# A mixture-of-experts stage whose first 28 experts add their results to the tokens in DRAM

## The chip, the cores and the metric

The kernel runs on one core of a Trainium2 chip. The metric is the device time in microseconds (us) of one execution. The core has TensorE (PE, matmuls; PEld is its weight load), VectorE (DVE), ScalarE (ACT), GpSimd (POOL) and SyncE (SP); SP issues nearly all transfers, GpSimd the indirect ones, and sixteen DMA engines carry them.

## What is computed

One encoder layer on 512 tokens of width 1024, in float32: a state-space mixer beside a latent attention, a cross-attention into 256 memory tokens, then a mixture of 32 gated experts, and a last norm. The change lies in the expert part:

```python
h = _rms(x, norm_moe_g[l])
x = x + _hier_moe(...)
return _rms(x, norm_final_g)

# _hier_moe, for the 512 tokens t = h:
#   the best of 4 groups, then the best 2 of the 8 experts of that group
eid = g_idx[:, None] * MOE_PER_GROUP + top_i
gates = jnp.sum(jax.nn.one_hot(eid, MOE_EXPERTS) * top_w[..., None], axis=1)
for g in range(MOE_GROUPS):
    sl = slice(g * MOE_PER_GROUP, (g + 1) * MOE_PER_GROUP)
    a = silu(einsum('td,edf->tef', t, w_gate[sl])) * einsum('td,edf->tef', t, w_up[sl])
    a = a * gates[:, sl, None]
    out = out + einsum('tef,efd->td', a, w_down[sl])
```

Each token has two experts. An expert has 3 MB of weights (gate and up 1024 x 256 each, down 256 x 1024), so the 32 experts have 96 MB, each byte read once.

## The kernel before

**Tiling.** The 32 experts are worked in 16 pairs n = 0..15. An expert has 64 places (`CAP`) for tokens; a pair fills the 128 partitions, its first expert in partitions 0 to 63, its second in 64 to 127. Tables worked out on the chip say for each place which token sits there (`TK`, and `IX` as integers; an empty place has a number out of range), with which weight (`GT`) and with which norm factor (`RS`). The stream X before this part lies in four SBUF tiles `X[t]` of 128 tokens x 1024 (called xr in the trace), and a copy of it lies in DRAM as `hd`, written by `logit_T` (L1322).

**One pair.** `gather(n)` (L1674) is an indirect DMA by GpSimd that brings the pair's rows of `hd` to `XG[n % 2]`; places out of range are skipped. `get` transposes them (pX), VectorE multiplies by the gain (XT). `first(n)` (L1755) runs 32 matmuls (pG) with gate and up, then silu on ScalarE (sl) and the product on VectorE (a). `second(n)` (L1793) transposes that (pA, aT), runs 16 matmuls with the down weights into two halves (pD), and writes the result times the gate weight as a pair of a high and a low half, `Y` (ScalarE L275, VectorE L276). It also makes `oht`, the 0/1 matrix that says which place belongs to which token.

**The sum.** Y stands by place, X by token. `combine` (L1814) takes two pairs at a time, n-2 and n-1 at each even n >= 2: for each of the four token tiles and two halves of the width four matmuls with `oht` sum high and low halves of both pairs in PSUM (pC), and VectorE adds that to X (L1824): 32 matmuls and 8 additions. Pairs 14 and 15 are summed in the end part by `last_sum` (L1859), followed by `fin_`: an addition per tile and half ("a"), its sum of squares and the root ("s"), the scaling and the store ("o"); `TO` (L66) is the order of these steps, shared out over VectorE, ScalarE and GpSimd.

**Weights and places.** Weights come in loads of 1 MB (gate and up of half an expert's width as two transfers, down as one) into a ring of SBUF places named by tags: earlier tiles of the layer (A, KV, H, Z, E, G), `NF` places F, and two places Y at first. `ring` (L1261) is the order in which places come round, `ahead` how many loads have a place before the first pair is done, `turn` the order of the first loads. `load_to(k)` issues loads up to the k-th on SP's queue; each waits until the place's last reader is done. `load_to` is called after each pair. `late` splits the last two down loads into halves of the width.

**What sets the order.** A scheduler orders the instructions on each engine by the program's order and its priorities, and adds the semaphore waits. `behind` pins one instruction behind another on an engine. On TensorE a pair's matmuls follow the pair before; between them stands the sum of two pairs.

Of the kernel before, what the change touches and what calls it, by code (L numbers as in the profile page):

```python
# [10 lines left out]
F32 = mybir.dt.float32  # L11
# [54 lines left out]
TO = 'a00 s00 a01 s01 a10 a11 o01 s10 o00 s11 a20 a21 o11 s20 o10 s21 a30 a31 o21 s30 s31 o20 o31 o30'.split()  # L66
# [18 lines left out]
NF = 1  # L85
# [11 lines left out]
GP = 0  # L97
TP = 0
# [5 lines left out]
def build(tc, I, out, dbg=None, stop=None):  # L104
# [872 lines left out]
    def ua(shape, dt, name):  # L977
        return A.tile(shape, dt, name=name, tag="A")
# [233 lines left out]
    hd = DR.tile([S, D], F32, name="hd")  # L1212
# [51 lines left out]
    tags += tuple(ring[i % len(ring)] for i in range(108 - ahead))  # L1264
    free = iter(tags[96:])

    turn = [5, 4, 20] + [i for i in range(ahead) if tags[i] not in "EFGY"]
    nheld = len(turn)
    turn += [6, 7] + list(range(ahead - NF, 96))

    def slot(tag, shape, name):
        if tag == "A":
            return ua(shape, F32, name)
        if tag in "EG":
            return (E[0] if tag == "E" else GP_).tile(shape, F32, name=name, tag=tag)
        if tag in "FY":
            return MP.tile(shape, F32, name=name, tag=tag, bufs=NF if tag == "F" else 2)
        return u(tag, shape, F32, name)
# [3 lines left out]
    def load_to(n):  # L1282
        while nld[0] < min(n, 96):
# [4 lines left out]
            after = nheld + 2 + FE < nld[0] <= ahead  # L1288
# [6 lines left out]
            else:  # L1295
# [3 lines left out]
                if i == 94:  # L1299
                    late.append((t, e))  # L1300
                    nc.sync.dma_start(t[:, :, 0:512], wdn[e][:, :, 0:512])
                elif i == 95:
                    late.append((t, e))
                    nc.sync.dma_start(t[:, :, 0:512], wdn[e][:, :, 0:512])
                    for t_, e_ in late:
                        nc.sync.dma_start(t_[:, :, 512:D], wdn[e_][:, :, 512:D])
                elif nld[0] == nheld + 2 + FE and FH:
                    nc.sync.dma_start(t[:, :, 0:512], wdn[e][:, :, 0:512])
                    held.append((t, e))
                else:  # L1310
                    nc.sync.dma_start(t, wdn[e])
            ew[e, c] = t

    late, gat, held = [], [], []
# [191 lines left out]
    load_to(nheld + 2 + min(FE, NF))  # L1506
# [67 lines left out]
    GT, RS = RC.tile([128, 16], F32, name="GT"), RC.tile([128, 16], F32, name="RS")  # L1574

# [17 lines left out]
    def weights(w, j):  # L1593
# [6 lines left out]
        v.tensor_tensor(fi[:, 1], w[:, :, 2], es_[:, cs], OP.not_equal)  # L1600
        v.tensor_tensor(fi, fi, w4[:, :, 0:2].rearrange("p n q -> p q n"), OP.mult)
# [78 lines left out]
    for t, e in held:  # L1680
        behind(nc.gpsimd.memset(t[0:1, 0, 512:513], 0.0), gat[-1])
        nc.sync.dma_start(t[:, :, 512:D], wdn[e][:, :, 512:D])
# [56 lines left out]
    silu = [None]  # L1739
# [53 lines left out]
    def second(n):  # L1793
# [6 lines left out]
        Y = MP.tile([128, 2, D], F32R, name=f"Y{n}", tag="Y")  # L1800
        oht = MP.tile([128, S], F32R, name=f"oht{n}", tag="oht")
        v.tensor_scalar(oht, tokh, TK[:, n:n + 1], None, OP.is_equal)
        stage["y", n] = Y, oht
        yield at_i
        for c in range(2):
# [6 lines left out]
            yield split(Y[:, 0, c * 512:c * 512 + 512], Y[:, 1, c * 512:c * 512 + 512], pd, GT[:, n:n + 1])[0]  # L1812

    def combine(ns, cs=(0, 1)):  # L1814
        for t in range(NT):
            for c in cs:
                ps = bank(f"pC{ns[0]}{t}{c}")
                for i, n in enumerate(ns):
                    Y, oht = stage["y", n]
                    for h in range(2):  # L1820
                        nc.tensor.matmul(ps, oht[:, t * 128:t * 128 + 128], Y[:, h, c * 512:c * 512 + 512],  # L1821
                                         start=i == 0 and h == 0, stop=i == len(ns) - 1 and h == 1)
                o = X[t][:, c * 512:c * 512 + 512]
                v.tensor_tensor(o, o, ps, OP.add)  # L1824

    fst = C.tile([128, 4, NT], F32, name="st_fin")
    for n in range(16):
# [19 lines left out]
        load_to(ahead + 4 - 2 * min(n, 1) + 6 * n - LS)  # L1847
        if n >= 2 and n % 2 == 0:
            combine((n - 2, n - 1))
# [26 lines left out]
    def fin_(k, t, c):  # L1876
        x = X[t][:, half[c]]
        r = fst[:, 3, t:t + 1]
        if k == "a":
            turn_("v", v.tensor_tensor(x, x, pc[t, c], OP.add))  # L1880
            if c == 0:
                nc.gpsimd.tensor_tensor(xg0[:, t], x, gf[:, half[0]], OP.mult)
# [6 lines left out]
        elif c:  # L1889
            turn_("v", v.reciprocal(r, r))  # L1890
            turn_("v", v.scalar_tensor_tensor(xg1[:, t], x, r, gf[:, half[1]], OP.mult, OP.mult))
            nc.sync.dma_start(out[0, t * 128:t * 128 + 128, half[1]], xg1[:, t])
        else:
            if FP >> t & 1:
                nc.gpsimd.tensor_scalar(xg0[:, t], xg0[:, t], r, 1.0, OP.mult, OP.mult)
            else:
                turn_("a", nc.scalar.activation(xg0[:, t], xg0[:, t], AF.Copy, scale=r))
            nc.sync.dma_start(out[0, t * 128:t * 128 + 128, half[0]], xg0[:, t])
# [29 lines left out]
```

## Time and profile before

| | |
|---|---|
| time, median of 3 runs (least to most) | 754.31 us (751.39 to 755.1) |
| the profiled execution | 754.67 us |
| its span, first to last instruction | 752.9 us |
| TensorE busy in the span, mean granted clock | 716.8 us (95%), 0.98 |
| VectorE, ScalarE, GpSimd busy | 450.3, 267.5, 76.6 us |
| DMA moved | 154.06 MB, mean 205 GB/s |
| chain that ended last: TensorE, VectorE, DMA | 77%, 13%, 3% |
| matmuls of the sums (L1821), in the chain | 53.8 us busy, 7% |

How to read it: the expert stage runs from about 484 us to the end, and the means over the span hide it. In its stretches one looks at TensorE's busy time and granted clock (1.00 is 2.4 GHz), at the DMA share (1.0: all sixteen engines busy) and at GB/s; then at the chain of waits, to see which of two busy resources the other waits for. Matmul times overlap, so a line's busy time is the union of its matmuls, not their number times their mean.

### The profile page before, as it was taken

The numbers are of one execution on the slowest core, as the hardware profiler recorded it, in microseconds if no ns is written. First come the engines' busy times: TensorE is split into PE (matmuls) and PEld (weight loads), VectorE is DVE, ScalarE is ACT, GpSimd is POOL, SyncE is SP. The second block draws the span as 40 slices with busy tenths as digits, with TensorE's granted clock in tenths as the row PEclk, the third lists the DMA queues.
The fourth block names the chain that finished last, engine by engine and source line by source line (L and its number), as shares of the span: only waits on it lengthen the run. The fifth ranks groups of instructions, "written<-read, shape, count | busy, mean of one in ns | idle before, by whom it ended". The sixth has DMA issues, their size and how long they took to land.

```text
span 752.9 us, 10637 instructions
## 1 busy us (share of the span) xinstructions
PE 716.8 (95%) x3900; PEld 504.7 (67%) x3900; DVE 450.3 (60%) x1018; ACT 267.5 (36%) x539; POOL 76.6 (10%) x135
## 2 busy tenths in 40 slices
PE   6999988997999999999999999999999999999994
PEld 4787777876688888888887888745353553535443
DVE  4799997955677878544557335545355543524245
ACT  5652255342756756434445222121112011111124
POOL 6200002013200000102000002200100001000003
PEclk9999999999989999999999999999999999999998
DMA  7673130543341533323258966599999999999003
GB/s 208 171 208 96 42 103 23 163 115 90 98 114 43 157 111 127 97 84 85 84 201 301 318 219 218 190 375 397 381 411 399 410 408 412 410 412 361 31 1 114
DMA packets 94592, 154.06 MB, mean 205 GB/s; under 512 B 29244, under 2 KB 61088, under 8 KB 90697
## 3 DMA queue, kind: packets, MB, share of 16 engines
q1 hardware_dynamic: 92120, 149.19, 56.6%
q0 software_dynamic: 2400, 4.15, 1.7%
q8 instruction: 32, 0.52, 0.3%
q14 instruction: 24, 0.19, 0.1%
q10 hardware_dynamic: 16, 0.00, 0.0%
HBM read 150.40 MB, written 6.82 MB: 209 GB/s over the span
## 4 chain that ended last, share of the span: by engine, by line
PE 77%; DVE 13%; DMA 3%; ACT 2%; issue 2%; SPq 1%; POOL 1%; ACTq 0%; DVEq 0%
PE pG L1763 15%; PE pD L1809 8%; PE pC L1821 7%; PE po L1023 2%; DVE lo L213 2%; PE pX L1430 2%; PE pX L1747 2%; PE pxq L267 2%; PE pxq L266 2%; PE pxq L265 2%; PE pxo L265 2%; PE pxo L266 2%; PE pxo L267 1%; PE pPT L1012 1%; DMA raw<-w_in 1%
## 5 line engine op out<-in xcount | busy, mean ns | idle before, releaser
L1763 PE MATMUL pG<-gu,XT 128*64 128x512 f32 x512 | 116.0, 596 | 0.0
L213 DVE TENSOR_TENSOR lo<-raw,hi 128x1024 fp32r<-128x1024 f32 (+3 forms) x64 | 75.8, 1189 | 59.7 <-ACT hi L203 59.3
L203 ACT ACTIVATE hi<-raw 128x1024 fp32r<-128x1024 f32 (+3 forms) x64 | 63.9, 1002 | 101.5 <-issue 21.5
L1763 PEld LDWEIGHTS pG<-gu,XT 128*64 128x64 f32 x512 | 35.5, 137 | 65.2 <-issue 63.4
L1782 ACT ACTIVATE sl<-pG,RS 128x256 f32<-128x256 f32 x16 | 7.6, 475 | 150.8 <-PE pG L1763 150.8
L1809 PE MATMUL pD<-dn,aT 128*64 128x512 f32 x256 | 60.6, 599 | 0.0
L1784 DVE SCALAR_TENSOR_TENSOR a<-pG,RS,sl 128x256 f32<-128x256 f32 x16 | 10.7, 671 | 74.3 <-ACT sl L1782 56.9
L1821 PE MATMUL pC<-Y,oht 128*128 128x512 f32 x224 | 53.8, 396 | 0.0
L1821 PEld LDWEIGHTS pC<-Y,oht 128*128 128x128 f32 x224 | 41.4, 188 | 15.0 <-issue 6.5
L1824 DVE TENSOR_TENSOR xr<-xr,pC 128x512 f32<-128x512 f32 x56 | 38.1, 686 | 6.7 <-PE pC L1821 6.7
L276 DVE SCALAR_TENSOR_TENSOR Y<-pD,GT,Y 128x512 fp32r<-128x512 f32 x32 | 24.0, 749 | 29.9 <-ACT Y L275 29.7
L275 ACT ACTIVATE Y<-pD,GT 128x512 fp32r<-128x512 f32 x32 | 22.0, 687 | 49.8 <-PE pD L1809 49.8
L1809 PEld LDWEIGHTS pD<-dn,aT 128*64 128x64 f32 x256 | 17.9, 136 | 30.4 <-issue 28.1
L1675 POOL DMA_INDIRECT XG<-hd,IX x15 | 15.5, 1032 | 189.1 <-PE pX L1747 185.1
L1404 DVE TENSOR_TENSOR XT<-pX,gmo 128x512 f32<-128x512 f32 x32 | 21.9, 686 | 12.4 <-PE pX L1747 8.3
L266 PE MATMUL pxq<-gT,hi 128*128 128x512 f32 x64 | 25.6, 400 | 0.0
L265 PE MATMUL pxq<-gT,hi 128*128 128x512 f32 x64 | 25.5, 399 | 0.0
L267 PE MATMUL pxq<-gT,lo 128*128 128x512 f32 x64 | 25.4, 396 | 0.0
L1747 PEld LDWEIGHTS pX<-ident,XG 128*128 128x128 f32 x120 | 16.2, 192 | 8.6 <-issue 7.3
L265 PE MATMUL pcq<-hT,hi 128*128 128x512 f32 x48 | 19.3, 402 | 2.8 <-DVE s_t L592 2.8
L266 PE MATMUL pq<-lo,cq 128*128 128x384 f32 x48 | 18.2, 379 | 2.3 <-DVE lo L213 2.3
L1007 ACT ACTIVATE P<-psc,sm 128x128 f32<-128x128 f32 (+3 forms) x32 | 16.8, 528 | 7.3 <-DVE sm L1006 7.1
(608 smaller groups left out, 1700.0 us busy)
## 6 DMA issues: line engine op xcount, KB each, us to landing
gu<-moe_w_gate SPq DMA_DIRECT2D x64, 512.0 KB
gu<-moe_w_up SPq DMA_DIRECT2D x64, 512.0 KB
dn<-moe_w_down SPq DMA_DIRECT2D x30, 1024.0 KB
raw<-w_in SPq DMA_DIRECT2D x9, 512.0 KB
raw<-xattn_w_v SPq DMA_DIRECT2D x8, 512.0 KB
raw<-xattn_w_k SPq DMA_DIRECT2D x8, 512.0 KB
raw<-w_out SPq DMA_DIRECT2D x8, 512.0 KB
raw<-xattn_w_q SPq DMA_DIRECT2D x8, 512.0 KB
```

The costliest lines, as they stand in the source:

```text
L203: anchor["act"] = nc.scalar.activation(hi, r, AF.Copy)
L213: anchor["dve"] = nc.vector.tensor_tensor(lo, r, hi.bitcast(F32), OP.subtract)
L265: i = nc.tensor.matmul(o, lh, rh, start=start, stop=False)
L266: nc.tensor.matmul(o, lh, rl, start=False, stop=False)
L267: anchor["pe"] = nc.tensor.matmul(o, ll, rh, start=False, stop=stop)
L275: i = nc.scalar.activation(hi, src, AF.Copy, scale=g)
L276: j = nc.vector.scalar_tensor_tensor(lo, src, g, hi.bitcast(F32), OP.mult, OP.subtract)
L1747: i = nc.tensor.transpose(ps[:, k * 128:k * 128 + 128], xg[:, 4 * c + k], ident)
L1763: i = nc.tensor.matmul(pg[64 * s:64 * s + 64], xt[c][:, kk, 64 * s:64 * s + 64], ew[2 * n + s, c][:, :, kk], start=k == 0, stop=k == 7)
L1809: i = nc.tensor.matmul(pd[64 * s:64 * s + 64], at_[:, f, 64 * s:64 * s + 64], ew[2 * n + s, 2][:, f, c * 512:c * 512 + 512], start=f == 0, ...
L1821: nc.tensor.matmul(ps, oht[:, t * 128:t * 128 + 128], Y[:, h, c * 512:c * 512 + 512], start=i == 0 and h == 0, stop=i == len(ns) - 1 and h ...
L1824: v.tensor_tensor(o, o, ps, OP.add)
```

## The change

The results of pairs 0 to 13 (`NS = 14`) no longer go through `oht` and TensorE. A second copy of X, `xd`, is written to DRAM beside `hd`. `second(n)` writes the result as one float32 half of a tile `YY` (ScalarE alone, no low half), and GpSimd issues two indirect DMAs with `compute_op=OP.add` that add the 128 rows to `xd`. Two, because a token may sit in both experts of a pair: the first takes the rows that are a token's first choice, the second those that are its second choice; `IY` holds the index lists, in which the other rows have a number out of range and are skipped. `combine` is gone. At n = 14 `take_back` reads `xd` into new tiles `xb`, which stand for X from then on. Pairs 14 and 15 are summed on TensorE as before.

X's four SBUF tiles hold weights meanwhile: two places X join the ring, `NF` is 2, and Y has one place for the first load in place of two. In the end part the scaling of the first halves moves from ScalarE and GpSimd to VectorE, and `TO` has another order.

```diff
-TO = 'a00 s00 a01 s01 a10 a11 o01 s10 o00 s11 a20 a21 o11 s20 o10 s21 a30 a31 o21 s30 s31 o20 o31 o30'.split()
+TO = 'a00 s00 a01 s01 a10 s10 a11 s11 o00 o01 a20 s20 a21 s21 o10 o11 a30 s30 a31 s31 o20 o21 o30 o31'.split()
...
-NF = 1
+NF = 2
...
+NS = 14
...
+    hd, xd = (DR.tile([S, D], F32, name=n) for n in ("hd", "xd"))
...
-    ring = ("A",) * 4 + ("E", "G") + ("A",) * (NA - 4) + ("KV",) * 4 + ("H",) * 2 + ("Z",) * 4 + ("E",) + ("F",) * NF
-    ahead = len(ring) + 2
-    tags = ring[:6] + ("Y",) * 2 + ring[6:]
+    ring = ("A",) * 4 + ("E", "G") + ("A",) * (NA - 4) + ("KV",) * 4 + ("H",) * 2 + ("Z",) * 4 + ("E",) + ("F",) * NF + ("X",) * 2
+    ahead = len(ring) + 1
+    nlate = sum(t in "FX" for t in ring)
+    tags = ring[:6] + ("Y",) + ring[6:]
...
+        nc.sync.dma_start(xd[t * 128:t * 128 + 128, n * 512:n * 512 + 512], xs)
...
+        if 2 * j < NS:
+            for w_ in range(2):
+                v.scalar_tensor_tensor(IY[:, w_, cs], fi[:, 1 - w_], EMPTY, TK[:, cs], OP.mult, OP.add)
...
-        Y = MP.tile([128, 2, D], F32R, name=f"Y{n}", tag="Y")
...
+            if not YY:
+                YY.append(slot("Y", [128, 2, D], "YY"))
+            Y = YY[0][:, n % 2]
...
+                yield nc.scalar.activation(Y[:, c * 512:c * 512 + 512], pd, AF.Copy, scale=GT[:, n:n + 1])
+        if not sums:
+
+            for w in range(2):
+                nc.gpsimd.indirect_dma_start(out=xd, out_offset=bass.IndirectOffsetOnAxis(ap=IY[:, w, n:n + 1], axis=0),
+                                             in_=Y, in_offset=None, bounds_check=S - 1, oob_is_err=False,
+                                             compute_op=OP.add)
...
-    def combine(ns, cs=(0, 1)):
...
+    def take_back():
+
         for t in range(NT):
...
+            if t % 2 == 0:
+                xb = slot(next(free), [128, 2, D], f"xb{t}")
+            nc.sync.dma_start(xb[:, t % 2], xd[128 * t:128 * t + 128])
+            X[t] = xb[:, t % 2]
...
-        if n >= 2 and n % 2 == 0:
-            combine((n - 2, n - 1))
+        if n == NS:
+            take_back()
...
+            if c == 0:
+                turn_("v", v.reciprocal(r, r))
+            xg = (xg0, xg1)[c]
+            turn_("v", v.scalar_tensor_tensor(xg[:, t], x, r, gf[:, half[c]], OP.mult, OP.mult))
```

The order of instructions shows it at three places. On GpSimd, in the middle of the stage, before the change (XG is what a gather fills; what a row waits for stands in brackets, PE, DVE and Activation being engines, DMASW0 to DMASW7 the landings of eight DMAs by GpSimd in turn):

```order
L1675 DMA XG_4703<-hd,IX 128x1024 [waits DMASW5_49,DMASW3_49,PE_49]
L1675 DMA XG_4702<-hd,IX 128x1024 [waits DMASW4_49,DMASW6_49,DVE_49,PE_49]
L1675 DMA XG_4703<-hd,IX 128x1024 [waits DMASW5_49,PE_49]
L1675 DMA XG_4702<-hd,IX 128x1024 [waits DMASW6_49,DVE_49,PE_49]
L1675 DMA XG_4703<-hd,IX 128x1024 [waits DMASW7_49,PE_49]
```

And after it (xd is the copy in DRAM, YY the result, IY the index lists):

```order
L1680 DMA XG_4713<-hd,IX 128x1024 [waits DMASW5_49,DMASW1_49,PE_49]
L1827 DMA xd<-YY,IY 512x1024 [waits DMASW6_49,DMASW4_49,Activation_49]
L1827 DMA xd<-YY,IY 512x1024 [waits DMASW6_49]
L1680 DMA XG_4712<-hd,IX 128x1024 [waits DMASW2_49,DVE_49,PE_49]
L1827 DMA xd<-YY,IY 512x1024 [waits DMASW7_49,Activation_49]
L1827 DMA xd<-YY,IY 512x1024 [waits DMASW1_49]
L1680 DMA XG_4713<-hd,IX 128x1024 [waits DMASW5_49,PE_49]
L1827 DMA xd<-YY,IY 512x1024 [waits DMASW2_49,Activation_49]
L1827 DMA xd<-YY,IY 512x1024 [waits DMASW4_49]
```

Between two gathers stand now the two additions of a pair: the first waits for ScalarE's YY and for the landing of the addition before it, the second for the landing of the first.

On TensorE, around the sum of pairs 0 and 1, before the change (dn is a down weight; two rows of down matmuls, then the first of 32 matmuls of the sum):

```order
L1809 MATMUL pD_5107<-dn_4678,aT_5095 64x512
L1809 MATMUL pD_5107<-dn_4680,aT_5095 64x512
L1821 MATMUL pC_5130<-Y_5003,oht_5004 128x512 x2
L1821 MATMUL pC_5130<-Y_5097,oht_5098 128x512 x2
L1821 MATMUL pC_5136<-Y_5003,oht_5004 128x512 x2
L1821 MATMUL pC_5136<-Y_5097,oht_5098 128x512
L1821 MATMUL pC_5142<-Y_5003,oht_5004 128x512
L1821 MATMUL pC_5136<-Y_5097,oht_5098 128x512
```

And after it:

```order
L1817 MATMUL pD_5134<-dn_4691,aT_5126 64x512
L1817 MATMUL pD_5134<-dn_4693,aT_5126 64x512
L1749 MATMUL pX_5170<-ident,XG_4713 128x128 x3
L1765 MATMUL pG_5162<-gu_4695,XT_5168 64x512
L1765 MATMUL pG_5162<-gu_4698,XT_5168 64x512
```

After the down matmuls of a pair follow the next pair's last transposes and its gate and up matmuls; the 32 matmuls of the sum are gone.

On SP, from the last weights on, before the change (novi is a count that is read into a register, fin the last gain, xg the output):

```order
L1301 DMA dn_6220<-moe_w_down 128x2x512
L1304 DMA dn_6222<-moe_w_down 128x2x512
L1306 DMA dn_6220<-moe_w_down 128x2x512
L1306 DMA dn_6222<-moe_w_down 128x2x512
L1707 TENSOR_LOAD novi
L1707 ISA x2
L1853 DMA fin<-norm_final_g 128x1024
L1898 DMA out<-xg_6534 128x512
L1892 DMA out<-xg_6535 128x512
```

And after it:

```order
L1304 DMA dn_6020<-moe_w_down 128x2x512
L1307 DMA dn_6022<-moe_w_down 128x2x512
L1309 DMA dn_6020<-moe_w_down 128x2x512
L1309 DMA dn_6022<-moe_w_down 128x2x512
L1709 TENSOR_LOAD novi
L1709 ISA x2
L1836 DMA xb_6172<-xd 128x1024 x2
L1836 DMA xb_6175<-xd 128x1024 x2
L1866 DMA fin<-norm_final_g 128x1024
L1905 DMA out<-xg_6246 128x512
L1905 DMA out<-xg_6247 128x512
```

Four reads of xd now stand ahead of the gain on SP's queue, and they wait for the last addition.

## Rows read from the trace of the kernel before

**Rows 1.** Stretches: length, busy us (instructions) by engine, granted clock, DMA share, GB/s.

```profile
core 0: us, PE busy (x) PEld busy (x) DVE busy (x) ACT busy (x) POOL busy (x), PEclk, DMA share, GB/s
...
519.10:550.60 31.50, 31.50 (x164) 15.77 (x164) 16.09 (x40) 4.63 (x10) 2.19 (x2) 1.00 1.00 394
...
614.00:645.50 31.50, 31.50 (x152) 14.97 (x148) 12.67 (x21) 4.30 (x8) 1.98 (x2) 1.00 1.02 412
```

**Rows 2.** Chain that ended last, 630 to 660 us: start, us, what.

```profile
634.48 7.02 PE pG L1763 x32
641.50 0.37 PE pA L1797 x2
641.87 0.55 PE pX L1747 x5
642.42 3.63 PE pD L1809 x16
646.05 7.50 PE pC L1821 x32
653.55 0.33 PE pX L1747 x3
```

**Rows 3.** Stretches, columns of rows 1: before the first pairs, after the weights.

```profile
484.00:487.00 3.00, 2.85 (x24) 1.07 (x23) 2.56 (x9) 0.00 (x0) 1.21 (x1) 1.00 0.00 0
487.00:490.00 3.00, 2.75 (x30) 0.99 (x26) 2.29 (x20) 0.31 (x2) 1.25 (x3) 1.00 0.67 221
...
694.00:696.00 2.00, 2.00 (x12) 0.64 (x10) 0.15 (x1) 0.69 (x1) 0.00 (x0) 1.00 0.36 135
```

**Rows 4.** DMA queues from 495 to 690 us: packets, MB, share of 16 engines.

```profile
q1 hardware_dynamic: 17387, 75.19, 97.2%
q0 software_dynamic: 1735, 3.06, 4.2%
```

**Rows 5.** The gathers' line, 495 to 690 us: ns, starts; us to landing.

```profile
L1675 POOL DMA_INDIRECT XG<-hd,IX x13: 989/992/1202, 495.3 to 685.7; - x13
...
DMA to landing us min/median/max: 6.7/7.8/8.8
```

**Rows 6.** The same line, 485 to 487 us, DMA engines idle.

```profile
DMA to landing us min/median/max: 4.6/4.6/4.6
```

**Rows 7.** Chain that ended last, whole span: a store, a load.

```profile
164.31 4.35 DMA kd<-s5k
...
173.74 3.19 DMA raw<-mla_w_kv_up
```

**Rows 8.** DMA issues of these two: engine, op, times, KB each.

```profile
raw<-mla_w_kv_up SPq DMA_DIRECT2D x4, 256.0 KB
...
kd<-s5k SPq DMA_DIRECT2D x4, 128.0 KB
```

**Rows 9.** Timeline from 505 us: start, us, engine, line, operation, idle before.

```profile
506.84 0.69 ACT L275 ACTIVATE Y<-pD,GT 128x512 fp32r<-128x512 f32 x1 [1.05 <-PE pD L1809]
...
507.57 0.99 POOL L1675 DMA_INDIRECT XG<-hd,IX  x1 [11.26 <-PE pX L1747]
```

**Rows 10.** Timeline from 708 us, columns of rows 9.

```profile
708.89 0.35 SPq L1853 DMA_DIRECT2D fin<-norm_final_g  x1
...
735.04 7.55 PE L1864 MATMUL pC<-Y,oht 128*128 128x512 f32 x32
...
744.48 0.68 DVE L1880 TENSOR_TENSOR xr<-xr,pC 128x512 f32<-128x512 f32 x1
...
745.08 0.15 DVE L1890 RECIPROCAL st_fin<-st_fin 128x1 f32<-128x1 f32 x1
...
746.47 0.75 DVE L1891 SCALAR_TENSOR_TENSOR xg<-xr,st_fin,fin 128x512 f32<-128x512 f32 x1
```

**Rows 11.** Stretches early in the span, columns of rows 1.

```profile
25.00:30.00 5.00, 3.89 (x13) 3.42 (x14) 2.18 (x12) 2.51 (x4) 2.11 (x6) 0.66 0.70 203
55.00:60.00 5.00, 2.24 (x12) 1.72 (x12) 4.93 (x28) 1.48 (x3) 0.00 (x0) 1.00 0.50 132
```

More of the change, by code (lines that the diff above doesn't have):

```diff
@@ L1260, in build, with slot @@
     order += parts(15, (2,))
[L1261 to L1264 removed]
+    ring = ("A",) * 4 + ("E", "G") + ("A",) * (NA - 4) + ("KV",) * 4 + ("H",) * 2 + ("Z",) * 4 + ("E",) + ("F",) * NF + ("X",) * 2
+    ahead = len(ring) + 1
+    nlate = sum(t in "FX" for t in ring)
+    tags = ring[:6] + ("Y",) + ring[6:]
+    tags += tuple(ring[i % len(ring)] for i in range(116 - ahead))
     free = iter(tags[96:])
[L1267 removed]
+    turn = [5, 4, 19] + [i for i in range(ahead) if tags[i] not in "EFGXY"]
     nheld = len(turn)
[L1269 to L1271 removed]
+    turn += [6] + list(range(ahead - nlate, 96))
+    def slot(tag, shape, name, dt=F32):
         if tag == "A":
[L1273 removed]
+            return ua(shape, dt, name)
         if tag in "EG":
[L1275 removed]
+            return (E[0] if tag == "E" else GP_).tile(shape, dt, name=name, tag=tag)
         if tag in "FY":
[L1277 to L1278 removed]
+            return MP.tile(shape, dt, name=name, tag=tag, bufs=NF if tag == "F" else 1)
+        return u("H" if tag == "X" else tag, shape, dt, name)
     nld = [0]
@@ L1287, in load_to @@
             tag = tags[i]
-            after = nheld + 2 + FE < nld[0] <= ahead
+            after = nheld + 1 < nld[0] <= ahead
             if c < 2:
@@ L1574, in build @@
     GT, RS = RC.tile([128, 16], F32, name="GT"), RC.tile([128, 16], F32, name="RS")
+    IY = RC.tile([128, 2, 16], I32, name="IY")
     def look_up(ohb, ps, j, cols, chain=False):
@@ L1799, in second @@
         at_i = nc.scalar.activation(at_, ps[:, 0:256].rearrange("p (f t) -> p f t", f=2), AF.Copy)
-        Y = MP.tile([128, 2, D], F32R, name=f"Y{n}", tag="Y")
-        oht = MP.tile([128, S], F32R, name=f"oht{n}", tag="oht")
-        v.tensor_scalar(oht, tokh, TK[:, n:n + 1], None, OP.is_equal)
-        stage["y", n] = Y, oht
+        sums = n >= NS
+        if sums:
+            Y = slot(next(free), [128, 2, D], f"Y{n}", F32R)
+            oht = MP.tile([128, S], F32R, name=f"oht{n}", tag="oht")
+            v.tensor_scalar(oht, tokh, TK[:, n:n + 1], None, OP.is_equal)
+            stage["y", n] = Y, oht
+        else:
+            if not YY:
+                YY.append(slot("Y", [128, 2, D], "YY"))
+            Y = YY[0][:, n % 2]
         yield at_i
@@ L1811, in second @@
                     in_turn(n, i)
-            yield split(Y[:, 0, c * 512:c * 512 + 512], Y[:, 1, c * 512:c * 512 + 512], pd, GT[:, n:n + 1])[0]
-    def combine(ns, cs=(0, 1)):
-        for t in range(NT):
[L1816 to L1824, printed above, removed]
+            if sums:
+                yield split(Y[:, 0, c * 512:c * 512 + 512], Y[:, 1, c * 512:c * 512 + 512], pd, GT[:, n:n + 1])[0]
+            else:
+                yield nc.scalar.activation(Y[:, c * 512:c * 512 + 512], pd, AF.Copy, scale=GT[:, n:n + 1])
[5 more added lines that the diff above has]
+    def take_back():
+        for t in range(NT):
+            if t % 2 == 0:
+                xb = slot(next(free), [128, 2, D], f"xb{t}")
+            nc.sync.dma_start(xb[:, t % 2], xd[128 * t:128 * t + 128])
+            X[t] = xb[:, t % 2]
     fst = C.tile([128, 4, NT], F32, name="st_fin")
@@ L1846, in build @@
             list(down)
[L1847 to L1849 removed]
+        load_to(ahead + 4 - min(n, 1) + 6 * n - LS)
+        if n == NS:
+            take_back()
     fin = slot(next(free), [128, 2, D], "fin")
@@ L1888, in fin_ @@
                 turn_("a", nc.scalar.activation(r, fst[:, 1, t:t + 1], AF.Sqrt, scale=1.0 / D, bias=fst[:, 2, t:t + 1]))
[L1889 to L1892, printed above, removed]
-        else:
[L1894 to L1898, printed above, removed]
+        else:
+            if c == 0:
+                turn_("v", v.reciprocal(r, r))
+            xg = (xg0, xg1)[c]
+            turn_("v", v.scalar_tensor_tensor(xg[:, t], x, r, gf[:, half[c]], OP.mult, OP.mult))
+            nc.sync.dma_start(out[0, t * 128:t * 128 + 128, half[c]], xg[:, t])
     list(down15)
```

15 lines of the change are left out of this document (3 added, 12 removed).

## The prediction

> **What bounds the kernel now.** I read the stretches of the expert stage first. From 519 us to 677 us TensorE is busy all the time at its upper level, 2.4 GHz, and the sixteen DMA engines are busy all the time too, at 394 to 412 GB/s [rows 1]. Two resources are full at once, so the next view must say which one waits for the other. The chain of waits does: two pairs, with the sum of both, run from one TensorE piece to the next with no DMA between them [rows 2]. Its pieces are 7.02 us (gate and up of a pair), 0.37 and about 1.0 us (transposes), 3.63 us (down), and 7.50 us for the sum of two pairs. A pair without the sum is 7.02 + 0.37 + 1.0 + 3.63 = 12.0 us; with half a sum it is 15.8 us. The weights are no bound at the end: DMA falls quiet at about 695 us [rows 3] and TensorE works on until 742.6 us [rows 10]. So TensorE sets the time, with the weights close behind.
>
> **The base.** The profiled execution took 754.7 us, 1.8 us more than its span of 752.9 us; the median of the runs shown is 754.3 us, so what is worked out against the profile stands for the median as well.
>
> **Removed: the sums on TensorE.** Seven sums of 7.50 us leave its path, with 56 additions on VectorE and the low halves of Y. TensorE alone would end the span at 752.9 - 52.5 = 700 us. The weights and the new path both end later, so this is a floor and not the forecast.
>
> **Moved: weights.** The freed places change the lead little. Before, 21 places are filled ahead of 484 us; now 20 are (one Y place serves YY), and then two F and two X places at about 487 us. DMA is idle from 484 to 487 us and at 0.67 from 487 to 490 us [rows 3]; filling the later gap is worth some 1.4 us, while one more load of 1.05 MB at 0.4 MB/us costs 2.6 us. The extra copy of X to xd (2.1 MB) is over before that idle stretch, which covers it; without the cover it would cost 5 us. The additions in DRAM are DMA work too. The gathers' queue needed 4.2% of 195 us for 3.06 MB, 2.7 us per MB [rows 4]. The reference has 512 tokens with two choices each, 64 rows for each of 16 pairs, so fourteen pairs add 14 x 64 rows of 4 KB, 3.67 MB: 9.8 us if an added row costs what a gathered row costs, 19.7 us if it is read and written as two transfers. The weights thus end at 695 + 2.6 - 1.4 + 9.8 = 706 us, up to 716 us; I take 706 us, as a gathered row is the nearest. TensorE, with 12.0 us a pair, frees places faster than that.
>
> **Added: 28 accumulating DMAs in one row.** This decides. The order on GpSimd shows each addition waiting for the one before it: the second of a pair for the first, the first of the next pair for the second of this one. Behind a waiting addition stand the later gathers, which have two pairs of lead; and ScalarE may write Y of pair n only when the additions of pair n-2 have landed. So 28 landings follow each other. The trace has a near relative of one: the gather, also 128 indices given by GpSimd with rows of 4 KB, of which about 64 are in range. From the start of its instruction (0.99 us) to its landing it takes 6.7 / 7.8 / 8.8 us (least, median, most) while the weights flow [rows 5], and 4.6 us with the DMA engines idle [rows 6]. An addition is not in the trace. From below it costs 4.6 us, even under the load; from above a gather and then a separate load, 7.8 + 3.2 [rows 7] = 11.0 us, as if its read and its write went one after another. What it has beyond a gather is a write that ends in DRAM, and the nearest rows for that are the store to kd, 4.35 us, against a load in 3.19 us [rows 7], though the load is twice as large [rows 8]: 1.16 us more. I take the gather plus 1.0 us: 8.8 us while weights flow and 5.6 us after, each with 0.1 us from landing to the next issue.
>
> The first addition stands behind the gather that ends on GpSimd at 508.6 us, and the first Y is written at 507.5 us [rows 9]; so the row starts at 508.6 us. Until 706 us there are 197.4 / 8.9 = 22.2 additions; the other 5.8 take 5.8 x 5.7 = 33.1 us. The last one lands at 739.1 us. At 17.8 us for a pair this is slower than the weights, which need 15.8 us now and 0.7 us more with the additions, so DMA is busy nearly all the time and the figure under load holds.
>
> The Trainium skill (DMA: Bandwidth & Descriptors, Anatomy of one DMA — SWDGE (gpsimd) path) fits 2.0 us plus bytes over 436 GB/s for a DMA issued by GpSimd; for 0.13 MB that is an estimate of 2.3 us, 28 times 64 us, and by it the additions would be hidden. The trace does not agree for a loaded core: 6.7 us was the shortest gather there [rows 5]. The same section says that a completion waits for the receipt of its write and that this is surprisingly long for HBM, which speaks against this change; by the 2 us that the page gives for HBM under high load (Latency and other measured facts), an estimate, the sum would be the 785 us worked out below for 2 us extra.
>
> **Added: the end.** X must come back. SyncE issues four reads of 0.5 MB and then the load of the last gain, which is issued at 708.9 us now, at leisure [rows 10], and then stands behind them, all after the last addition. With 3.2 us for a load [rows 7] and 0.52 MB / 0.41 = 1.3 us for each further one, X arrives at +3.2, 4.5, 5.8 and 7.1 us and the gain at +8.4 us. Meanwhile VectorE adds four halves; left are four additions of 0.68 us, eight scalings of 0.75 us (four of them came from ScalarE and GpSimd) and four reciprocals of 0.15 us [rows 10]: 9.3 us. From VectorE's last scaling, which ends at 747.2 us, to the end of the span are 5.7 us. Together 8.4 + 9.3 + 5.7 = 23.4 us. TensorE's last sums (7.55 us) lie beside the additions; without that cover they would add at most that. The span is 739.1 + 23.4 = 762.5 us, and the forecast 762.5 + 1.8 = **764.3 us**, 1.3% over the profiled execution. With 0.5 us beyond a gather in place of 1.0 us the same sum gives 754.6 us: break-even is a landing of 8.3 us under load.
>
> **The rivals.**
> Additions as short as gathers (faster). 197.4 / 7.9 = 25.0 by 706 us, the other 3.0 in 14.1 us, then the end: 745 us. For it: each carries half the rows of a gather. Against it: a gather writes no DRAM, and the store took 1.16 us longer than the load. It decides below 8.1 us; its cases reach from 735 to 751 us.
> The weights set the end (faster). If landings are under 6.9 us, all 28 are over by 706 us. After the last weights come eight down matmuls (1.8 us), the 17.9 us from 735.0 us to the end, and some 2 us more on VectorE, with 1.8 us outside the span: 729 us, or 740 us with the weights at 716 us. For it: DMA is already full [rows 1]. Against it: only a gather at idle DMA is that short.
> Read and write one after another (slower still). With 2 us extra: 19.9 by 706 us, 8.1 x 6.7 = 54 us after, 785 us; with 3.2 us extra 812 us. For it: an addition must have the old row before it can write. Against it: sixteen DMA engines share the rows.
> TensorE's clock (slower). It would stand idle 5.8 us in each 17.8 us. In the trace 5 us with 3.89 us busy were granted 0.66 on the mean, so part of them ran at 1.2 GHz, and others with 2.24 us busy 1.00 [rows 11]. It decides only if nearly half of the 12.0 us per pair ran at 1.2 GHz, so that a pair passes 17.8 us; with all of it there a pair takes 24 us, and sixteen of them from 490 us on end past 870 us.
> That the freed places do nothing for the time is in the forecast: they are worth the 1.4 us above, since weights are not on the path.
>
> **How the numbers follow.** Half a per cent is about what a measurement of this kernel can tell from no change: 750.5 to 758.1 us is the same, which is a landing of 8.1 to 8.5 us. Forecast, a landing between 8.1 and 9.8 us under load: 0.50, of which 0.15 lie within that half per cent. As short as gathers: 0.22. Weights: 0.10. One after another: 0.15. Clock: 0.03. So faster 0.32, same 0.15, slower 0.53. The range leaves out most of the weights' case below and the longer half of the one-after-another case above: 735 to 797 us.
>
> **What would show it.** Right: on GpSimd the additions follow each other at 8 to 9.5 us until about 706 us and at 5 to 6.5 us after; ScalarE's waits before YY name a DMA; DMA goes quiet at 700 to 716 us; the last addition is issued near 733 us; TensorE is idle a third of the stage; xb is read in the last 25 us and VectorE waits there for the gain. Wrong: a median from issue to landing under 8 us or over 10 us, or gaps in the row of additions that another engine ends.

## The result and the profile after

The changed kernel takes **762.97 us** (median; 761.73 to 765.45), the kernel before beside it 754.45 us: a ratio of 1.0123, 95% interval 1.0098 to 1.0148. That is slower by more than the half per cent that counts as a difference here, and 1.3 us under the forecast of 764.3 us. The profiled execution took 763.0 us, 1.8 us more than its span, as before. The page has TensorE at 90% of the span and names a new wait on two engines (columns: busy us and share; then a group's count, busy us, mean ns, idle time ahead of it and what ended that):

```profile
span 761.2 us, 10197 instructions
...
PE 685.8 (90%) x3676; PEld 472.0 (62%) x3676; DVE 392.3 (52%) x938; ACT 263.8 (35%) x537; POOL 114.7 (15%) x160
...
L1823 ACT ACTIVATE YY<-pD,GT 128x512 f32<-128x512 f32 x28 | 18.1, 685 | 161.0 <-DMA xd<-YY,IY 151.6
L1827 POOL DMA_INDIRECT xd<-YY,IY x28 | 44.5, 1588 | 167.0 <-DMA xd<-YY,IY 148.4
```

GpSimd stands 167 us in front of its 28 additions and ScalarE 161 us in front of YY; 148 and 152 us of that end with the landing of an addition. Where the chain before went from one TensorE piece to the next [rows 2], it now reads, from 540 to 690 us, summed by line (what it calls "issue" lies between the two additions of a pair, where GpSimd's timeline names the landing of the first; the shares pass 100% because pieces at the ends reach out of the stretch):

```profile
by line: DMA xd<-YY,IY 53.0%; issue 42.4%; POOL xd L1827 9.5%; POOLq L1680 0.3%; POOLq L1827 0.3%
```

The stretches (columns of rows 1) say what that did to the others, first in the kernel before, then in the changed one. TensorE, not idle there before, is idle 17.3 of 128 us; the DMA engines are as full as before:

```profile
core 0: us, PE busy (x) PEld busy (x) DVE busy (x) ACT busy (x) POOL busy (x), PEclk, DMA share, GB/s
540.00:668.00 128.00, 128.00 (x624) 60.91 (x622) 58.15 (x120) 17.70 (x35) 8.52 (x9) 1.00 1.02 409
```

```profile
540.00:668.00 128.00, 110.73 (x480) 41.32 (x478) 23.39 (x67) 14.27 (x31) 29.49 (x21) 0.95 1.02 394
```

```profile
700.00:710.00 10.00, 5.64 (x17) 1.96 (x14) 1.35 (x2) 1.91 (x4) 1.58 (x1) 0.81 0.85 294
710.00:720.00 10.00, 10.00 (x42) 3.80 (x42) 0.84 (x2) 1.54 (x3) 3.11 (x2) 0.85 0.18 33
```

All but 0.2 of the 17.3 us end with the landing of a gather, as TensorE's line for the transposes says (540 to 668 us; line, count, busy us, mean ns, idle time ahead and what ended it). The gathers come late because on GpSimd they stand behind additions that wait:

```profile
L1749 PE MATMUL pX<-ident,XG 128*128 128x128 f32 x64 | 12.0, 316 | 17.1 <-DMA XG<-hd,IX 17.1
```

The row itself, first the additions' line between 540 and 692 us (instruction ns, first and last start; then issue to landing), then GpSimd's timeline for the last six:

```profile
L1827 POOL DMA_INDIRECT xd<-YY,IY x17: 1554/1578/1585, 545.7 to 686.6; - x17
...
DMA to landing us min/median/max: 7.6/8.5/9.0
```

```profile
704.92 1.58 POOL L1827 DMA_INDIRECT xd<-YY,IY  x1 [7.23 <-ACT YY L1823]
712.25 1.56 POOL L1827 DMA_INDIRECT xd<-YY,IY  x1 [5.74 <-DMA xd<-YY,IY]
718.35 1.55 POOL L1827 DMA_INDIRECT xd<-YY,IY  x1 [4.55 <-DMA xd<-YY,IY]
722.80 1.57 POOL L1827 DMA_INDIRECT xd<-YY,IY  x1 [2.90 <-DMA xd<-YY,IY]
728.83 1.56 POOL L1827 DMA_INDIRECT xd<-YY,IY  x1 [4.46 <-ACT Y L276]
734.09 1.55 POOL L1827 DMA_INDIRECT xd<-YY,IY  x1 [3.70 <-DMA xd<-YY,IY]
```

Seventeen starts in 140.9 us are a **step of 8.81 us** while weights flow. From 704.92 to 734.09 us, as the weights end, the mean step is 5.83 us. Two of these waits carry ScalarE's name, but the YY that each needed had been written by 687.3 and 719.0 us; what they waited for was the landing before, which came at 704.0 and 728.1 us. The chain of the end (start, us, what) closes the account:

```profile
734.09 4.99 DMA xd<-YY,IY
739.08 0.02 SPq L1836
...
741.00 7.46 DMA fin<-norm_final_g
...
755.62 0.61 DVE xg L1904
```

The last addition lands at 739.08 us, the gain at 748.46 us, and VectorE's last scaling ends at 756.2 us. TensorE's last sums, held up by the late gathers, end at 738.90 us: at the end two paths that both begin in the row are level.

### The profile page after: what moved, and what is told of

Same layout as the page of the kernel before. It is cut to its first block, busy times and chain, and to the rows that moved or that the text cites. A ratio compares the mean times of both kernels' runs of the same rounds, so it can differ in the third digit from the quotient of the medians.

```text
span 761.2 us, 10197 instructions
## 1 busy us (share of the span) xinstructions
PE 685.8 (90%) x3676; PEld 472.0 (62%) x3676; DVE 392.3 (52%) x938; ACT 263.8 (35%) x537; POOL 114.7 (15%) x160
## 4 chain that ended last, share of the span: by engine, by line
PE 47%; DMA 17%; issue 14%; DVE 14%; POOL 3%; ACT 2%; SPq 2%; POOLq 0%; DVEq 0%; ACTq 0%
DMA xd<-YY,IY 12%; POOL xd L1827 3%; PE pG L1765 2%; PE po L1024 2%; DVE lo L214 2%; PE pX L1431 2%; PE pxq L268 2%; PE pxq L267 2%; PE pxq L266 2%; PE pxo L266 2%; DMA raw<-w_in 1%; PE pxo L267 1%; PE pPT L1013 1%; PE pxo L268 1%; DMA XG<-hd,IX 1%
## 5 line engine op out<-in xcount | busy, mean ns | idle before, releaser
L1765 PE MATMUL pG<-gu,XT 128*64 128x512 f32 x512 | 126.3, 595 | 0.0
L1817 PE MATMUL pD<-dn,aT 128*64 128x512 f32 x256 | 82.0, 645 | 0.0
L1765 PEld LDWEIGHTS pG<-gu,XT 128*64 128x64 f32 x512 | 40.2, 136 | 65.5 <-issue 63.8
L1823 ACT ACTIVATE YY<-pD,GT 128x512 f32<-128x512 f32 x28 | 18.1, 685 | 161.0 <-DMA xd<-YY,IY 151.6
L1827 POOL DMA_INDIRECT xd<-YY,IY x28 | 44.5, 1588 | 167.0 <-DMA xd<-YY,IY 148.4
L1405 DVE TENSOR_TENSOR XT<-pX,gmo 128x512 f32<-128x512 f32 x32 | 22.1, 691 | 48.9 <-PE pX L1749 43.2
L1749 PE MATMUL pX<-ident,XG 128*128 128x128 f32 x120 | 22.6, 317 | 27.2 <-DMA XG<-hd,IX 27.2
L1817 PEld LDWEIGHTS pD<-dn,aT 128*64 128x64 f32 x256 | 23.1, 146 | 38.1 <-issue 36.5
L266 PE MATMUL pcq<-hT,hi 128*128 128x512 f32 x48 | 19.3, 402 | 2.8 <-DVE s_t L593 2.8
L268 PE MATMUL pcq<-hT,lo 128*128 128x512 f32 x48 | 19.2, 400 | 0.0
L267 PE MATMUL pcq<-hT,hi 128*128 128x512 f32 x48 | 19.1, 397 | 0.0
```

What stands on the lines that cost most here:

```text
L266: i = nc.tensor.matmul(o, lh, rh, start=start, stop=False)
L267: nc.tensor.matmul(o, lh, rl, start=False, stop=False)
L268: anchor["pe"] = nc.tensor.matmul(o, ll, rh, start=False, stop=stop)
L1405: return v.tensor_tensor(xt, ps.rearrange("p (k t) -> p k t", k=4), gmo[:, 4 * c:4 * c + 4, None].to_broadcast([128, 4, 128]), OP.mult)
L1749: i = nc.tensor.transpose(ps[:, k * 128:k * 128 + 128], xg[:, 4 * c + k], ident)
L1765: i = nc.tensor.matmul(pg[64 * s:64 * s + 64], xt[c][:, kk, 64 * s:64 * s + 64], ew[2 * n + s, c][:, :, kk], start=k == 0, stop=k == 7)
```

## The experiments

**My theory**: 28 landings in one row set the time; weights come next. **Rivals**: the additions' transfers take DMA time from the weights (bytes); the reading back and the gain set the loss (end); late gathers, the freed places or TensorE's clock. One table first. "Last weights" is when SyncE issues the last two pieces of weights, in the timeline of each run; "last addition" is its issue. The ratio is to the kernel before on the same chip. Plain writes and empty additions rest on two executions each (736.63 and 742.04 us; 736.83 and 737.45 us), the others on four to ten. Times within a run are those of its profiled execution, in which the expert stage began up to 4.8 us earlier or later than in another; where that matters it is said.

| kernel | us | ratio (95%) | last weights | last addition |
|---|---|---|---|---|
| before | 754.45 | | 683.15 | |
| changed | 762.97 | 1.0123 (1.0098 to 1.0148) | 697.50 | 734.09 |
| no additions | 719.25 | 0.9534 (0.9501 to 0.9568) | 682.20 | |
| empty additions | 737.14 | 0.9777 (0.9748 to 0.9806) | 683.15 | 708.95 |
| plain writes | 739.34 | 0.9810 (0.9775 to 0.9845) | 693.23 | 714.10 |
| first choices only | 731.45 | 0.9700 (0.9681 to 0.9720) | 693.13 | 694.74 |
| gain early | 759.16 | 1.0074 (1.0056 to 1.0092) | 696.48 | 733.4 |
| two copies | 751.92 | 0.9981 (0.9963 to 0.9999) | 704.30 | 705.50 |
| two copies, better end | 748.44 | 0.9922 (0.9893 to 0.9950) | 705.97 | 706.5 |
| the same, second written | 740.24 | 0.9828 (0.9798 to 0.9858) | 695.64 | 698.57 |
| the same, joins shared | 743.33 | 0.9855 (0.9838 to 0.9873) | 697.67 | 698.9 |
| eight pairs | 761.32 | 1.0097 (1.0066 to 1.0127) | 699.93 | 641.3 |
| six pairs | 760.73 | 1.0084 (1.0055 to 1.0112) | 696.70 | 607.1 |
| eight pairs, two copies | 753.60 | 0.9987 (0.9970 to 1.0005) | 706.30 | 598.5 |

### Half the row, and two rows

```
-            for w in range(2):
+            for w in range(1):
```

> The additions of the tokens' second choices are left out: 14 additions instead of 28, everything else as in the changed kernel. Serial row (my theory): 14 landings of about 9 us need 127 us of the 197 us that the weights flow, so the row no longer sets anything; ScalarE hardly waits for an addition before YY, the gathers of pairs 5 to 15 are no longer late, the last addition lands near 715 us instead of 739.1, and the device time falls to 730 to 744 us. Bytes (rival: the additions cost what their transfers take from the weights): half of their bytes go, 5 to 10 us of DMA time, so 753 to 758 us. End part (rival: reading back and the gain set the loss): hardly any change, 759 to 763 us.

Measured: 731.45 us, within the theory's 730 to 744 us; neither half of the bytes, for which 753 to 758 us were expected, nor the end explains a fall of 31.5 us. The row is no longer in the way: its 14 additions are spread from 508.5 to 694.7 us, and ScalarE's waits before YY, 62.4 us, all name TensorE.

```
+    xd1 = DR.tile([S, D], F32, name="xd1")     # zeros, near 295 us
-                nc.gpsimd.indirect_dma_start(out=xd, ...
+                nc.gpsimd.indirect_dma_start(out=(xd, xd1)[w], ...
...
+    for x, x1 in zip(X, XC):                   # ahead of the last pair's split
+        v.tensor_tensor(x, x, x1, OP.add)
```

> First choices are added to one copy of the tokens in DRAM, second choices to another that begins as zeros (written near 250 us); both are read back at the end and added on VectorE. All 28 additions and all their bytes stay, 4 MB of traffic come on top, but the two additions of a pair no longer wait for each other. Serial row (my theory): two rows of 14 landings, 9 to 11 us each, 126 to 154 us long, neither sets anything; the device time falls to 735 to 750 us, TensorE waits for weights instead of additions. Bytes (rival): more bytes than before, so 764 to 772 us. Late gathers or TensorE's clock as the true cause (rival): little change, 757 to 766 us.

Measured: 751.92 us. With all 28 additions and 4 MB more the kernel is 11 us faster than the changed one, so the bytes did not make the difference. Late gathers this run cannot tell from the row: with two rows no matmul waits for a gather any more. That they are the row's effect and not its cause, the changed kernel's chain says: from 540 to 690 us neither the landing of a gather nor TensorE stands in it. A kernel that issues its gathers ahead of the waiting additions was not run. The time lies 2 us over the theory's range. Two things were not in it: the last weights came at 704.30 us, and TensorE's last sums waited 4.77 us for VectorE, which had the copies to join first and stood 8.9 us before its first join for a read of the second copy.

### What a landing is made of

```
-                                             compute_op=OP.add)
+                                             compute_op=OP.bypass)
```

> The 28 indirect DMAs overwrite the tokens' rows instead of adding to them; same rows, bytes written, order and waits (left out: the addition itself). If adding makes a landing longer than a plain transfer of the same rows (I had put 1.0 us on it, gather against addition), a landing falls from 8.7 us to between 6.5 and 7.7 us while weights flow, the row runs ahead of the weights and the time falls to 740 to 752 us. If a landing is queueing and the wait for the write's receipt, it stays at 8 to 9.5 us, and the time at 759 to 764 us.

```
-                v.scalar_tensor_tensor(IY[:, w_, cs], fi[:, 1 - w_], EMPTY, TK[:, cs], OP.mult, OP.add)
+                v.tensor_scalar(IY[:, w_, cs], TK[:, cs], EMPTY, None, OP.add)
```

> All 28 additions are issued with every row out of range, so that nothing is added (left out: the additions' whole work); the order, the waits and the 28 landings in a row stay. The first runs put 0.80 us of DMA time on an addition (last weights asked for at 693.1 us with 14, at 704.3 us with 28) and 0.40 us on a plain write. If that price is the rows' traffic (my theory), the last weights are asked for near 682 to 686 us, a landing is the empty row's fixed cost of 2 to 5 us, and the time falls to 720 to 733 us. If it is the cost of 28 separate requests whatever they carry (rival), the last weights stay at 692 us or later, a landing at 7 us or more, and the time at 738 us or more.

The additions' line from 540 to 692 us, of the plain writes and then of the empty additions:

```profile
L1827 POOL DMA_INDIRECT xd<-YY,IY x19: 978/996/1256, 543.8 to 685.9; - x19
...
DMA to landing us min/median/max: 6.7/7.3/7.9
```

```profile
L1827 POOL DMA_INDIRECT xd<-YY,IY x19: 1553/1578/1585, 541.3 to 685.8; - x19
...
DMA to landing us min/median/max: 6.8/7.7/8.5
```

Plain writes land in 7.3 us and follow each other every 7.89 us; the time is 739.34 us, just under what was expected if adding makes the landing longer. It does: 8.81 against 7.89 us a step. But 0.6 of these 0.9 us are GpSimd's instruction, 1.58 us for an addition and 1.00 us for a plain write: while weights flow, the first packet of a pair's second addition moves about 4.8 us after the instruction's start, that of a plain write 4.2 us. The empty additions, which move no row, surprised me: every **8.03 us**, where I had expected 2 to 5 us and the rival 7 us or more, so here the rival was right. On the weights my theory held: they are asked for at 683.15 us, as if no addition were there. The time, 737.14 us, lies between the two expectations. What the 8 us are, the end of the same row shows, on GpSimd's timeline when the weights are over:

```profile
702.49 1.57 POOL L1827 DMA_INDIRECT xd<-YY,IY  x1 [1.43 <-DMA xd<-YY,IY]
705.98 1.56 POOL L1827 DMA_INDIRECT xd<-YY,IY  x1 [1.92 <-DMA xd<-YY,IY]
708.95 1.55 POOL L1827 DMA_INDIRECT xd<-YY,IY  x1 [1.41 <-DMA xd<-YY,IY]
```

There an empty addition takes 3.0 to 3.5 us a step. So of the 8.03 us some 5 are spent only beside the weights' traffic, whatever the request carries, and some 3 are fixed. Rows and adding together put 0.8 us on a step under load, and more when the weights are over: 5.83 us in the changed kernel. An empty request is not empty for the DMA engines: the trace has 144 packets of 4 or 8 bytes for each. Its first packet moves 4.8 us after the start of the instruction while weights flow and 2.1 us when they are over; so some 2.7 of the 5 us pass before any packet moves. Why was not taken apart further.

### What the additions cost the weights

```
-            for w in range(2):
+            for w in range(0):
```

> The 28 additions are not issued at all (left out; the tokens are still read back and the last two pairs still summed). This is what freeing TensorE of 14 pairs' sums is worth when their replacement costs nothing. If the additions' price is DMA time plus the row (my theory), the last weights are asked for near 682 us, the end follows 38 us behind as it did behind 14 additions (693.1 to 730.9), and the time is 719 to 726 us: the gain of 28 to 35 us that the row and the traffic of the additions then take back. If the freed places or TensorE's clock cost something of their own (rival), the last weights are asked for at 690 us or later and the time is 730 us or more.

Measured: 719.25 us, as expected, and the last weights at 682.20 us. The chain that ended last has no TensorE in it until the last weights are there, at 691 us (from 540 to 700 us, by line):

```profile
by line: DMA gu<-moe_w_up 72.1%; DMA dn<-moe_w_down 25.2%; PE pD L1817 4.5%; PE pC L1877 0.8%; PE pA L1799 0.2%; issue 0.2%; SPq L1311 0.0%
```

So the freed places and TensorE's clock cost nothing that shows, and the price of the additions comes in two parts. **DMA time**: SyncE's last pieces of weights, of no additions, of 14, of 28 plain writes and of 28 additions in two rows (start, us, engine, line):

```profile
682.20 1.82 SPq L1309 DMA_DIRECT2D dn<-moe_w_down  x2
```

```profile
693.13 1.82 SPq L1309 DMA_DIRECT2D dn<-moe_w_down  x2
```

```profile
693.23 1.81 SPq L1309 DMA_DIRECT2D dn<-moe_w_down  x2
```

```profile
704.30 1.81 SPq L1316 DMA_DIRECT2D dn<-moe_w_down  x2
```

Part of these differences is the start of the stage. One piece of GpSimd's work ahead of it shows that, in the runs with no additions and with plain writes (columns as above, then the operation and the idle time before it):

```profile
474.26 0.61 POOL L1549 TENSOR_TENSOR XG<-r_rk,slots 128x256 f32<-128x256 f32 x1 [5.38 <-ACT r_rk L1425]
```

```profile
476.26 0.61 POOL L1549 TENSOR_TENSOR XG<-r_rk,slots 128x256 f32<-128x256 f32 x1 [5.38 <-ACT r_rk L1425]
```

In the other two it starts at 474.42 and 474.60 us. Counted from there, 14 additions cost 10.8 us and 28 cost 21.8 us, 0.77 and 0.78 us each; 28 plain writes cost 9.0 us, 0.32 us each. An addition costs 2.4 times a plain write of its rows. The rules for kernel authors in the Trainium skill (DMA: Bandwidth & Descriptors, Rules for kernel authors) say that an accumulating DMA reads its destination and writes it later; the two prices fit that, with something over. **The row**: empty additions take no DMA time that shows (last weights at 683.15 us) and still end 17.9 us later than none. Real ones in one row end another 25.8 us later: weights asked for 14 us later (697.50 us), a step of 8.81 instead of 8.03 us, so that 22 additions and not 25 are issued by 700 us, and a row that then goes on at 5.8 instead of 3.0 to 3.5 us a step. How these share the 25.8 us was not measured.

### The end, and a kernel that beats both

```
+            fin = slot(next(free), [128, 2, D], "fin")     # ahead of take_back()
+            nc.sync.dma_start(gf, ...)
```

> The last gain is loaded ahead of the reading back instead of behind it, so it has landed long before the last addition. Serial row with an end part of VectorE work (my theory): the first scaling starts about 3 us sooner, VectorE's adds, reciprocals and scalings follow without a gap, 2.0 to 3.0 us less: 760.0 to 761.0 us, 1.008 to 1.009 of the kernel before. If the four reads set the end part, nothing changes: 763 us, 1.012.

Measured: 759.16 us, 3.8 us less, a little under the 760.0 to 761.0 us expected; the last addition was issued 0.7 us earlier in that run, so some 3 us are the gain's. VectorE's timeline shows no wait between its reciprocal and the first scaling, which waited for the gain from 746.7 to 748.6 us in the changed kernel:

```profile
741.59 2.61 DVE L1894 TENSOR_TENSOR xb<-xb,pC 128x512 f32<-128x512 f32 x4 [10.35 <-DMA xb<-xd]
744.24 0.16 DVE L1903 RECIPROCAL st_fin<-st_fin 128x1 f32<-128x1 f32 x1
744.43 1.42 DVE L1905 SCALAR_TENSOR_TENSOR xg<-xb,st_fin,fin 128x512 f32<-128x512 f32 x2
```

The next three start from two copies, with the gain early and the copies joined behind the last pair's split. First the second choices are plain writes (a token has one second choice, and its row holds zeros):

```
-                                             compute_op=OP.add)
+                                             compute_op=(OP.add, OP.bypass)[w])
```

> Two copies, as before; the second choices overwrite their rows of zeros instead of adding to them (each token has one second choice, so the sum is the same), the last gain is loaded ahead of the reading back, and the two copies are added behind the last pair's split on VectorE instead of ahead of it. Price by the two sizes (my theory): 14 x 0.80 + 14 x 0.40 = 16.8 us of DMA time instead of 22.4, the last weights asked for near 699 us instead of 704.3, and an end that no longer waits with TensorE for the second copy: 739 to 745 us. If the additions' price does not halve for a plain write, or the reading back of 4 MB sets the end, 747 to 752 us.

> As the two copies with plain writes of the second choices, but the second choices are added again: it tells what of the 11.7 us between the first kernel with two copies and the one that writes is the cheaper transfer, and what is the end (gain ahead, copies joined later). By 14 x 0.40 us for the transfer: 5.6 us slower than the one that writes, 744 to 748 us, last weights asked for near 701 to 704 us. If only the end mattered: 739 to 742 us. If only the transfer mattered: 749 to 753 us.

Measured: 740.24 us with writes, **1.7% faster than the kernel before** (ratio 0.9828), and 748.44 us with additions, just over the expected 744 to 748 us. The last weights come at 695.64 and 705.97 us; of these 10.3 us 4.4 are the whole stage, which began that much earlier in the one profiled execution (first addition at 505.6 against 509.9 us), and 6.0 are the transfer, where I had worked out 5.6. By this, a plain write costs 0.35 us beside an addition's 0.78. The end alone is worth 3.5 us, from 751.92 to 748.44 us.

```
-            v.tensor_tensor(x[:, half[c]], x[:, half[c]], x1[:, half[c]], OP.add)
+            (v, nc.gpsimd)[c].tensor_tensor(...)
```

> As the two copies with plain writes of the second choices, but of the eight 128x512 additions that join the two copies at the end four are done on GpSimd instead of VectorE. VectorE's row at the end (16 us from 717 us, with the eight joins in it) loses 4 x 0.65 us; if it sets the end, 736.5 to 739 us; if GpSimd's joins (1.3 us or more each) come late for VectorE's adds, 740 to 743 us.

Measured: 743.33 us, no gain, and just over the upper of the two expectations. GpSimd takes 1.29 to 1.76 us for a join, and VectorE's next add waits for it:

```profile
720.01 1.28 DVE L1904 TENSOR_TENSOR xb<-xb,pC 128x512 f32<-128x512 f32 x2 [1.18 <-POOL xb L1925]
```

### Fewer pairs

I then tried to balance the engines: the first pairs by additions, the others by sums as before (`NS = 8` or `6`, the tokens read back after pair `NS + 1` into two places that weights give up).

> Only pairs 0 to 7 are added by DMA, the tokens are read back after pair 9 into two places that weights then no longer use, and pairs 8 to 15 are summed by one-hot matmuls as in the kernel before. Row theory with the DMA price: the row of 16 landings ends near 655 us, far from the end; 16 x 0.80 = 12.8 us plus 5 us of reading back put the last request for weights near 700 us; TensorE's part, 7.5 us less for each two pairs, would end near 713 us, so the weights lead by a little: 733 to 742 us. If TensorE's sums, squeezed in while it already waits for weights, lengthen its chain (rival): 745 to 752 us.

> As the one with eight pairs, with pairs 0 to 5 added by DMA and 6 to 15 summed. By the same sum: 12 x 0.80 = 9.6 us and 5 us of reading back, last weights near 697 us; TensorE's part near 720 us; the two are level, 732 to 740 us. Rival as there: 745 to 752 us.

Measured: 761.32 and 760.73 us; both expectations missed by 20 us, beyond the rival's too. My sum took 7.5 us of TensorE work off for each two pairs, as if TensorE could keep what it saves. The stretch of the kernel with eight pairs, and pieces of its chain after the row:

```profile
540.00:668.00 128.00, 107.57 (x468) 43.35 (x468) 26.05 (x67) 14.90 (x33) 27.27 (x20) 0.93 1.02 395
```

```profile
641.26 8.58 DMA xd<-YY,IY
649.98 0.69 ACT Y L276
...
651.51 4.38 PE pC L1839 x11
...
741.15 5.28 PE pC L1892 x22
```

TensorE idles 20.4 us beside the row, which passes a pair in two steps of about 8.8 us, 17.6 us, where TensorE in the kernel before needs 15.8 us with half a sum [rows 2]. After the row the chain is nearly all TensorE's to the end, with sums again. The row spends early what the missing sums save. If that is so, two rows must give it back:

> As the one with eight pairs, but first and second choices go to two copies, so that the 16 additions stand in two rows; both copies are read back after pair 9 (two more places leave the weights' use) and joined on VectorE ahead of the first sums. With one row, TensorE idled 20 us between 540 and 668 us, and then had sums to do until 748.7 us. If that idling was the row (two steps of 8.8 us for a pair, against 15.4 us of TensorE work with sums), it shrinks to about 9 us, as it was with two copies and 28 additions (9.4 us there in the same stretch), and the end comes 5 to 12 us sooner: 749 to 756 us. If the sums behind the row lengthen TensorE's chain whatever the row does (rival), 758 us or more.

Measured: 753.60 us, in the expected range, with 13.6 us of TensorE idle in that stretch (9 had been expected; part of the rest is a wait for the second copy):

```profile
540.00:668.00 128.00, 114.36 (x498) 45.30 (x497) 32.57 (x77) 16.08 (x32) 25.15 (x19) 0.97 1.02 393
```

So it was the row, and not the sums behind it. It is no faster than before: the weights are asked for 23 us later (706.30 us), and TensorE still has half the sums.

## Why the prediction was right, point by point

**The bound and the floor.** TensorE with "the weights close behind" was right. No additions at all give 719.25 us, and what then ends last is weights. Taking 52.5 us off TensorE was worth 35 us; with these weights and this end, replacing these sums can give no more.

**The weights' price was mis-sized.** The additions as DMA work stood in the sum at 9.8 us, as gathered rows (0.35 us each), with 19.7 us as the upper end. Measured: 0.78 us each, 22 us for 28. The term failed because the nearest row was the wrong kind: an addition cost 2.4 times a plain write of its rows. It did little harm, and that was luck: in one row only 22 additions were issued by 700 us, and the freed places cost nothing where I had put 1.2 us, so the weights ended near 708 us instead of 706 us (the DMA share falls from 0.85 to 0.18 about there).

**The row.** First addition at 509.15 us (forecast 508.6); a step of 8.81 us (8.9); the 23rd issued at 704.92 us (22.2 additions by 706 us); 5.83 us a step after it (5.7); last landing at 739.08 us (739.1). The step is a landing of 8.5 us (8.8) and 0.3 us to the next issue (0.1). The 1.0 us over a gather came out right for a wrong reason. I had it from a store that ends in DRAM. But a plain write, which ends there too, follows at 7.89 us, a gather's pace. Of the 0.9 us that an addition has on top, 0.6 are GpSimd's instruction, which I had put at a gather's 0.99 us and which takes 1.58; the other 0.3 come with the adding. That the size agreed is luck.

**The end** took 761.2 - 739.1 = 22.1 us (23.4), and it waited for the gain, as forecast. TensorE's last sums did lie beside the additions, but only just: they ended 0.18 us before the last landing. The load of the gain took longer than worked out (landed 9.4 us after the last addition landed, not 8.4), the work after it less (7.6 us, not 9.3), and the tail 5.0 us (5.7).

**What did not show.** TensorE was to be idle a third of the stage; it was 13.5% from 540 to 668 us. In that stretch its down matmuls (line, count, busy us, mean ns; the changed kernel, then the one before)

```profile
L1817 PE MATMUL pD<-dn,aT 128*64 128x512 f32 x128 | 42.0, 665 | 0.0
```

```profile
L1809 PE MATMUL pD<-dn,aT 128*64 128x512 f32 x128 | 29.2, 598 | 0.0
```

take 12.8 us more for as many. Part of that is the clock, 0.95 on the mean. Behind a wait of 5.45 us for a gather it was 0.50 (1.2 GHz) from 584 to 590 us, and a pair's 16 down matmuls took 5.97 us instead of 3.63 [rows 2]:

```profile
584.13 1.31 PE L1749 MATMUL pX<-ident,XG 128*128 128x128 f32 x5 [5.45 <-DMA XG<-hd,IX]
585.37 5.97 PE L1817 MATMUL pD<-dn,aT 128*64 128x512 f32 x16
```

That waiting hides in the rest of the busy time is not shown. The clock rival did not set the time: no addition up to 690 us waited for TensorE, and its last sums were done when the last addition landed. With 0.18 us between them, it was close.

**The rivals.** "As short as gathers" forecast 745 us for a step of 7.9 us; the plain writes had 7.89 us and took 739.34 us, so that sum, too, was 6 us off and on the safe side. Break-even between the two kernels lies, by these runs, between a step of 7.9 and one of 8.8 us, as the 8.3 us of landing said; the plain writes also take less DMA time, so it is not located more closely. "One after another" fell: an addition has 0.9 us over a plain write, not 2 to 3.2.

## What to carry to other kernels

Where work leaves a full engine for a chain of DMAs, price first the number of landings in a row, times a landing measured under the load that the stage has. Then ask what the engine can win before the next resource sets the end (here 35 of 52.5 us), and what the new transfers take from that resource: here an accumulating DMA took 2.4 times a plain write. Ask also what stands behind the waiting DMAs on the issuing engine; here it was the gathers, and through them the row reached TensorE. Where additions must follow each other only because they share a destination, two destinations make two rows, and a plain write into zeros was here less than half the price of an addition.

## What the runs showed of the hardware

- Indirect DMAs with every row out of range follow each other every 8.03 us while weights flow at a DMA share of 1.03, and every 3.0 to 3.5 us when they are over. Each still puts 144 packets of 4 or 8 bytes on the DMA engines; the first moves 4.8 us after the start of the instruction under load and 2.1 us without.
- The accumulating indirect DMA occupies GpSimd for 1.58 us, with or without rows in range; the plain one takes 1.0 us.
- A request that adds its rows (3.44 MB in 28 requests, some 30 rows of 4 KB each) takes 0.77 to 0.78 us of DMA time from the weights, one that writes them 0.32 to 0.35 us: 2.2 to 2.4 times.
